# Modulation vectors summed on GpSimd instead of TensorE, and roots by Newton's steps on VectorE, in a two-layer decoder trunk

## The chip, the cores and the metric

One core of a Trainium2 chip runs the whole kernel. The metric is the device time of one execution in microseconds (us): the median of three runs, with the lowest and the highest beside it. PE is TensorE's matmul pipe, PEld its weight loads, DVE is VectorE, ACT is ScalarE, POOL is GpSimd, and SP is the engine that issues the DMAs.

## The reference

The trunk has two layers of three sublayers each, over one sequence of 256 tokens of width 1024, all in float32. Sublayers 0 and 2 of a layer are gated feed-forward products (FFN), sublayer 1 is a gMLP mixer in layer 0 and block-sparse attention in layer 1.

```
mod  = silu(c) @ mod_w[i] + mod_b[i]                 # 9 vectors of 1024 for layer i: shift, scale, gate of 3 sublayers
h    = rmsnorm(x, norm_g[i, s]) * (1 + scale) + shift
x   += 0.5 * gate * ((silu(h @ w_gate) * (h @ w_up)) @ w_out)        # s = 0, 2
x   += gate * mixer(h)                                               # s = 1
rmsnorm(x, g) = x / sqrt(mean(x*x) + 1e-6) * g
```

A vector of `mod` is the product of one row (1024 numbers) with a 1024 x 1024 matrix. There are 18 of them; each must be ready before the sublayer that uses it begins (shift, scale) or ends (gate).

## The kernel before

The 256 tokens are two tiles of 128 (t = 0 and t = 1). A float32 product is made of three float32r products: each weight tile is split on the chip into a high half (a cast on ACT) and a low half (a subtraction on DVE), and the pieces high x high, high x low and low x high are added up in PSUM. So each 128 x 1024 weight tile `hl_*` costs one cast (line 182), one subtraction (line 183) and 12 matmuls of 512 columns (line 204). The tiles `hl` share a ring of 8 buffers, so ACT and DVE can run up to 8 tiles ahead of PE and not further.

A modulation vector is a unit of background work, `mod_unit(i, s, part)`: part 0 is the shift, 1 the scale, 2 the gate. Four calls (pieces) each load 1 MB of `mod_w` and do two multiply-adds on DVE (line 117) into `ma`, a 128 x 1024 accumulator; a fifth call, `reduce`, adds up the 128 partitions of `ma` and spreads the sum over all partitions as the tile `bc`. Of the 18 vectors two are made in another way at the start of the program, which leaves 16 units. `tick` takes one call from the list `background`; `gemm` ticks after every fourth weight tile (or as its argument `ticks` says). Between the sublayers stands a hand-over: the last product's sum goes through `residual` (tiles `y`, `x`), `row_rstd` (`ss`, `mx`, the root `rx`), and `ada` (`h`), is transposed on PE (`tr_h`), and becomes `hTh` (cast, ACT) and `hTl` (subtraction, DVE), the left side of the next product. While t = 0 goes through it PE has the last 36 matmuls of t = 1; while t = 1 goes through it PE has the first matmuls of the next product for t = 0.

The program is written down in one order, and a list scheduler of the language sets the order on each engine from it. It may take an instruction that was written later if it thinks the engine free. So pieces of units that were written later stand on DVE wherever the scheduler saw room.

Of the kernel before, what the change touches and what calls it, by code (L numbers as in the profile page):

```python
# [36 lines left out]
LEAD = 6  # L37
BLOCKS = ((0, 128), (128, 128), (256, 256), (512, 256), (768, 256))
# [20 lines left out]
def trunk(ctx: ExitStack, tc: tile.TileContext, x, c, rel_bias, mod_w, mod_b, norm_g,  # L59
# [31 lines left out]
    halves_ = const.tile([P, P], F32R, name="halves")  # L91
    nc.gpsimd.memset(halves_.bitcast(F32), 0.5)
# [5 lines left out]
    def mod_unit(i, s, part):  # L98
# [22 lines left out]

        def reduce():
            hl = hl_slot([P, 2, D], F32R, f"mhl{i}{s}{part}")
            nc.scalar.copy(hl[:, 0, :], st["acc"])
            nc.vector.tensor_sub(hl[:, 1, :], st["acc"], hl[:, 0, :].bitcast(F32))
            if part == 1:
                g = pool.tile([P, 2, D], F32, tag="mraw", name=f"g{i}{s}", bufs=2)
                nc.sync.dma_start(g[:, 0, :], norm_g[i, s:s + 1, :].to_broadcast([P, D]))
            bc = pool.tile([P, D], F32, tag="bc", name=f"bc{i}{s}{part}", bufs=3)
            lhs = halves_ if part == 2 and s != 1 else ones  # L130
            for h in range(2):
                ps = tr_bank(f"mps{i}{s}{part}{h}")
                sl = slice(h * 512, h * 512 + 512)
                for j in range(2):
                    nc.tensor.matmul(ps, lhs, hl[:, j, sl], start=j == 0, stop=j == 1)  # L135
                if part == 1:
                    nc.vector.scalar_tensor_tensor(bc[:, sl], ps, 1.0, g[:, 0, sl],
                                                   op0=ALU.add, op1=ALU.mult)
                else:
                    nc.scalar.copy(bc[:, sl], ps)  # L140
            vec[i, s, part] = bc

        return [piece(k) for k in range(0, KD, 2)] + [reduce]

    vec = {}
    background = []

    def tick(n=1):
        for _ in range(n):
            if background:  # L150
                background.pop(0)()
# [5 lines left out]
    def split_weights(src, key, kt, cols):  # L157
# [25 lines left out]
        nc.vector.tensor_sub(hl[:, 1, :w], r[:, kt % 2, :w], hl[:, 0, :w].bitcast(F32))  # L183
# [90 lines left out]
    def inverse_root(m, name):  # L274
        r = small(f"r{name}")
        nc.gpsimd.tensor_tensor(r, m, mhalf, op=ALU.pow)
        return r
# [25 lines left out]
    def residual(i, s, t, ps):  # L303
        for h in range(2):
# [3 lines left out]
            nc.vector.tensor_add(x_sb[t][:, sl], x_sb[t][:, sl], y)  # L308
# [101 lines left out]
    def ffn(i, s):  # L410
# [3 lines left out]
        for n, w in enumerate((1024, 1024, 768)):  # L414
# [3 lines left out]
            else:  # L418
                g = product(w_in, f"g{i}{s}{n}", two(c0, w), h_lhs,
                            lead_first=LEAD if n == 0 else 0, lead_last=2)  # L420
# [257 lines left out]
    def gmlp(i, s):  # L678
# [282 lines left out]
```

## Time and profile before

| | us |
|---|---|
| median of 3 runs (lowest to highest) | 1143.95 (1143.52 to 1146.61) |
| time of the profiled execution | 1144.84 |
| span of the profiled execution | 1143.0 |
| PE busy | 1125.2 |
| PEld busy | 938.3 |
| DVE busy | 820.5 |
| ACT busy | 593.5 |
| POOL busy | 33.0 |

The span is what the profile covers; the time of the same execution is 1.8 us longer, and lies 0.9 us above the median of the three runs. Busy time is the union of an engine's instructions; matmuls overlap in the pipe, so PE's busy time is not a sum of their durations.

### The profile page before, as it was taken

Reading aid. Unit: us, or ns where it says so; the run is one execution under the profiler, and the core shown is the slowest. Engines: PE = TensorE matmul, PEld = TensorE weight load, DVE = VectorE, ACT = ScalarE, POOL = GpSimd, SP = SyncE. Lnnn points to the kernel's source line nnn. Section 1 sums busy time; section 2 is a strip of 40 time slices with the busy share of each in tenths; the row PEclk is TensorE's granted clock in tenths of the full one; section 3 lists DMA queues with packets and bytes.
Section 4 is the critical chain, followed back from the end, with each engine's and each line's share of the span. In section 5 each row is a group of like instructions: output and inputs, shape, how many; then the busy total and the mean of one; then the engine's idle time right before and its main releaser. Section 6 shows DMA issues by size and latency. Waiting matters only on the chain.

```text
span 1143.0 us, 14125 instructions
## 1 busy us (share of the span) xinstructions
PE 1125.2 (98%) x5429; PEld 938.3 (82%) x5429; DVE 820.5 (72%) x988; ACT 593.5 (52%) x853; POOL 33.0 (3%) x43
## 2 busy tenths in 40 slices
PE   8999999999999999999999999999999999999997
PEld 5688988778888887888988788998877778889985
DVE  3798687855797888584778867577888877644653
ACT  4565554456555544563553555455457557554541
POOL 1000000000000000000000000000000000000000
PEclk9999999999999999999999999999999999999999
DMA  9988787647698595775869558487877556455630
GB/s 315 329 312 308 284 329 276 238 155 270 230 334 318 211 337 194 289 258 174 289 254 360 175 184 308 147 323 259 292 262 271 203 184 218 151 184 158 217 141 37
DMA packets 88738, 279.47 MB, mean 244 GB/s; under 512 B 5240, under 2 KB 17616, under 8 KB 88672
## 3 DMA queue, kind: packets, MB, share of 16 engines
q1 hardware_dynamic: 88672, 278.58, 68.9%
q8 instruction: 42, 0.69, 0.2%
q14 instruction: 24, 0.20, 0.0%
HBM read 277.49 MB, written 1.07 MB: 244 GB/s over the span
## 4 chain that ended last, share of the span: by engine, by line
PE 85%; DVE 7%; DMA 3%; ACT 2%; issue 1%; POOL 1%; SPq 0%; POOLq 0%; DVEq 0%; ACTq 0%
PE ps_o L204 23%; PE ps_u L204 19%; PE ps_g L204 18%; PE ps_gu L204 6%; PE ps_v L204 5%; DMA mw<-in_mod_w_dram 3%; PE ps_qk L204 3%; PE ps_g L532 2%; PE ta L389 2%; DVE ma L117 1%; PE mps L135 1%; PE sv L750 1%; PE ps_u00b L204 1%; DVE hl_g L183 1%; PE ps_u00a L532 1%
## 5 line engine op out<-in xcount | busy, mean ns | idle before, releaser
L204 PE MATMUL ps_o<-hl_o,ahl 128*128 128x512 f32 x1440 | 334.1, 391 | 1.0 <-ACT ahl L345 1.0
L204 PEld LDWEIGHTS ps_o<-hl_o,ahl 128*128 128x128 f32 x1440 | 269.1, 188 | 56.3 <-ACT ahl L345 1.2
L182 ACT CAST hl_o<-raw_o 128x1024 fp32r<-128x1024 f32 x120 | 125.7, 1055 | 112.1 <-PE ps_o L204 71.8
L183 DVE TENSOR_TENSOR hl_o<-raw_o,hl_o 128x1024 fp32r<-128x1024 f32 x120 | 145.9, 1222 | 52.7 <-ACT hl_o L182 51.9
L204 PE MATMUL ps_g<-hl_g,hTh 128*128 128x512 f32 (+1 forms) x704 | 183.4, 371 | 0.0
L204 PE MATMUL ps_u<-hl_u,hTh 128*128 128x512 f32 (+1 forms) x704 | 181.5, 369 | 0.0
L117 DVE SCALAR_TENSOR_TENSOR ma<-mw,cs,ma 128x1024 f32<-128x1024 f32 x128 | 165.5, 1294 | 17.5 <-DMA mw<-in_mod_w_dram 16.9
L204 PEld LDWEIGHTS ps_u<-hl_u,hTh 128*128 128x128 f32 x704 | 129.6, 188 | 17.6
L204 PEld LDWEIGHTS ps_g<-hl_g,hTh 128*128 128x128 f32 x704 | 129.2, 188 | 17.5 <-ACT hTh L285 0.2
L183 DVE TENSOR_TENSOR hl_u<-raw_u,hl_u 128x1024 fp32r<-128x1024 f32 (+1 forms) x88 | 98.4, 1126 | 60.0 <-ACT hl_u L182 58.8
L183 DVE TENSOR_TENSOR hl_g<-raw_g,hl_g 128x1024 fp32r<-128x1024 f32 (+1 forms) x88 | 97.6, 1124 | 50.8 <-ACT hl_g L182 50.5
L182 ACT CAST hl_g<-raw_g 128x1024 fp32r<-128x1024 f32 (+1 forms) x88 | 83.3, 974 | 94.8 <-PE ps_u L204 84.1
L182 ACT CAST hl_u<-raw_u 128x1024 fp32r<-128x1024 f32 (+1 forms) x88 | 85.3, 974 | 59.1 <-PE ps_g L204 54.6
L204 PE MATMUL ps_g<-hl_g,hTl 128*128 128x512 f32 (+1 forms) x352 | 110.3, 372 | 0.0
L204 PE MATMUL ps_u<-hl_u,hTl 128*128 128x512 f32 (+1 forms) x352 | 108.6, 369 | 0.0
L204 PEld LDWEIGHTS ps_u<-hl_u,hTl 128*128 128x128 f32 x352 | 65.4, 188 | 8.7
L204 PEld LDWEIGHTS ps_g<-hl_g,hTl 128*128 128x128 f32 x352 | 65.0, 188 | 9.1 <-issue 0.6
L204 PE MATMUL ps_gu<-hl_gu,hTh 128*128 128x512 f32 x192 | 55.0, 394 | 0.0
L204 PE MATMUL ps_v<-hl_v,hTh 128*128 128x512 f32 x192 | 54.2, 392 | 0.3 <-ACT hl_v L182 0.3
L183 DVE TENSOR_TENSOR hl_v<-raw_v,hl_v 128x1024 fp32r<-128x1024 f32 x24 | 28.8, 1221 | 22.7 <-ACT hl_v L182 22.7
L204 PEld LDWEIGHTS ps_v<-hl_v,hTh 128*128 128x128 f32 x192 | 35.8, 188 | 8.4 <-ACT hl_v L182 0.5
L204 PEld LDWEIGHTS ps_gu<-hl_gu,hTh 128*128 128x128 f32 x192 | 35.8, 188 | 7.1
(173 smaller groups left out, 1249.0 us busy)
## 6 DMA issues: line engine op xcount, KB each, us to landing
mw<-in_mod_w_dram SPq DMA_DIRECT2D x64, 1024.0 KB, 7.1
raw_o<-in_ffn_w_out_dram SPq DMA_DIRECT2D x44, 1024.0 KB, 4.8
raw_g<-in_ffn_w_in_dram SPq DMA_DIRECT2D x28, 1024.0 KB, 5.1
raw_u<-in_ffn_w_in_dram SPq DMA_DIRECT2D x28, 1024.0 KB, 5.0
raw_g<-in_ffn_w_in_dram SPq DMA_DIRECT2D x16, 768.0 KB, 4.5
raw_u<-in_ffn_w_in_dram SPq DMA_DIRECT2D x16, 768.0 KB, 4.4
raw_v<-in_gmlp_w_in_dram SPq DMA_DIRECT2D x12, 1024.0 KB, 7.7
raw_gu<-in_gmlp_w_in_dram SPq DMA_DIRECT2D x12, 1024.0 KB, 7.1
```

The source lines that it names most:

```text
L117: nc.vector.scalar_tensor_tensor(st["acc"], w[:, j, :], cs[:, k0 + j:k0 + j + 1], st["acc"], op0=ALU.mult, op1=ALU.add)
L135: nc.tensor.matmul(ps, lhs, hl[:, j, sl], start=j == 0, stop=j == 1)
L182: nc.scalar.copy(hl[:, 0, :w], r[:, kt % 2, :w])
L183: nc.vector.tensor_sub(hl[:, 1, :w], r[:, kt % 2, :w], hl[:, 0, :w].bitcast(F32))
L204: nc.tensor.matmul(ps[t, h][:, :cw], lhs(k, t)[p], hls[k][:, wp, o:o + cw], start=k == 0 and p == 0 and wp == 0, stop=k == nk - 1 and p == 1)
L389: nc.tensor.transpose(ps[:, j * P:(j + 1) * P], src[:, j * P:(j + 1) * P], ident)
L532: nc.tensor.matmul(prod[n][t, h], h_lhs(k, t)[part], hls[n, k][:, wp, h * 512:h * 512 + 512], start=k == 0 and part == 0 and wp == 0, stop ...
L750: nc.tensor.matmul(sv[:, sl], wsT[:, g, :], v[n][:, t, lo - n * D:hi - n * D], start=True, stop=True)
```

## The change

Of the 16 reductions over partitions, 13 go from TensorE to GpSimd: two `partition_all_reduce` instructions of 128 x 512 each read `ma` and write `bc`, in place of a cast on ACT, a subtraction on DVE, four matmuls with a matrix of ones, and two copies out of PSUM. For the scale (part 1) one multiply-add on DVE follows, over 128 x 1024. The three units named in `ON_PE` keep the matmuls; they are the ones that are worked on within the attention. The factor 0.5 of the FFN gates moves from the matrix of halves into `residual`.

The root `1/sqrt` was a power on GpSimd (line 276). It stays so at the program's two ends (`AT_ENDS`); the other 12 become eight small DVE instructions: a first guess from the bits, and three Newton steps.

No unit is ticked in the first product after a hand-over (`ticks=KD + 1`, in FFNs and the gMLP), and the DVE instructions of the 13 units may not stand ahead of the latest weight split written before them (`issue_after`), while those of the three other units may.

```diff
+ON_PE = ((1, 1, 2), (1, 2, 0), (1, 2, 1))
+AT_ENDS = ("x000", "x001", "fin0", "fin1", "last")
...
         def reduce():
+            bc = pool.tile([P, D], F32, tag="bc", name=f"bc{i}{s}{part}", bufs=3)
+            for h in range(2):
+                sl = slice(h * 512, h * 512 + 512)
+                nc.gpsimd.partition_all_reduce(bc[:, sl], st["acc"][:, sl], P, ReduceOp.add)
+            if part == 1:
+                nc.vector.scalar_tensor_tensor(bc, bc, 1.0, norm_row(), op0=ALU.add, op1=ALU.mult)
+            vec[i, s, part] = bc
+
+        def reduce_pe():
             hl = hl_slot([P, 2, D], F32R, f"mhl{i}{s}{part}")
             nc.scalar.copy(hl[:, 0, :], st["acc"])
             nc.vector.tensor_sub(hl[:, 1, :], st["acc"], hl[:, 0, :].bitcast(F32))
...
-        return [piece(k) for k in range(0, KD, 2)] + [reduce]
+        pe = (i, s, part) in ON_PE
+        return [(f, not pe) for f in
+                [piece(k) for k in range(0, KD, 2)] + [reduce_pe if pe else reduce]]
...
             if background:
-                background.pop(0)()
+                f, held_back = background.pop(0)
+                with ExitStack() as stack:
+                    if held_back:
+                        stack.enter_context(tc.issue_after(split["last"].ins))
+                    f()
...
-        nc.vector.tensor_sub(hl[:, 1, :w], r[:, kt % 2, :w], hl[:, 0, :w].bitcast(F32))
+        split["last"] = nc.vector.tensor_sub(hl[:, 1, :w], r[:, kt % 2, :w],
+                                             hl[:, 0, :w].bitcast(F32))
...
     def inverse_root(m, name):
-        r = small(f"r{name}")
-        nc.gpsimd.tensor_tensor(r, m, mhalf, op=ALU.pow)
+
+        if name in AT_ENDS:
+            r = small(f"r{name}")
+            nc.gpsimd.tensor_tensor(r, m, mhalf, op=ALU.pow)
+            return r
+        r, mh, t = (small(f"{a}{name}") for a in ("r", "mh", "rt"))
+        nc.vector.tensor_scalar(r.bitcast(I32), m.bitcast(I32), -0.5, float(0x5F3759DF),
+                                op0=ALU.mult, op1=ALU.add)
+        nc.vector.tensor_scalar_mul(mh, m, -0.5)
+        for _ in range(3):
+            nc.vector.scalar_tensor_tensor(t, r, mh, r, op0=ALU.mult, op1=ALU.mult)
+            nc.vector.scalar_tensor_tensor(r, t, 1.5, r, op0=ALU.add, op1=ALU.mult)
         return r
...
-            nc.vector.tensor_add(x_sb[t][:, sl], x_sb[t][:, sl], y)
+            nc.vector.scalar_tensor_tensor(x_sb[t][:, sl], y, 0.5 if s != 1 else 1.0,
+                                           x_sb[t][:, sl], op0=ALU.mult, op1=ALU.add)
...
-                            lead_first=LEAD if n == 0 else 0, lead_last=2)
+                            lead_first=LEAD if n == 0 else 0, lead_last=2,
+                            ticks=4 if n else KD + 1)
```

The order on GpSimd, in the gMLP and the FFN after it (layer 0; the first digit in a name is the layer, the second the sublayer, the third the part or the tile). Before:

```order
L106 MEMSET ma012_1877 128x1024
L106 MEMSET ma020_2304 128x1024
L276 TENSOR_TENSOR rx010_1749<-mx010_1747,mhalf_82 128x1
L276 TENSOR_TENSOR rx011_1834<-mx011_1832,mhalf_82 128x1
L686 AFFINE_SELECT ws_2050<-ws_2050 128x2048
```

And after the change, where each `ISA` row with `bc` is a pair of all-reduces:

```order
L133 ISA bc011_1642<-ma011_1385 128x512 x2
L108 MEMSET ma020_2471 128x1024
L720 AFFINE_SELECT ws_2029<-ws_2029 128x2048
L133 ISA bc012_2416<-ma012_2066 128x512 x2
L108 MEMSET ma021_3043 128x1024
L133 ISA bc020_2886<-ma020_2471 128x512 x2
```

The powers are gone from the queue, and every unit's accumulator is cleared only after the pair of the unit two before it, whose buffer it takes over.

On DVE, at the hand-over into the attention (from layer 1's first FFN to its sublayer 1; `y10`, `x1` are residuals of the FFN, `h11`, `rx11`, `hl_qk0` belong to the attention's first product). Before, from the first residual of t = 0 to its `h`:

```order
L307 TENSOR_TENSOR y1000_6357<-ps_o10_00_5987,bc102_5383 128x512
L308 TENSOR_TENSOR x0_69<-x0_69,y1000_6357 128x512
L117 SCALAR_TENSOR_TENSOR ma120_6558<-mw1206_6731,cs_71,ma120_6558 128x1024 x2
L307 TENSOR_TENSOR y1001_6360<-ps_o10_01_5993,bc102_5383 128x512
L293 TENSOR_TENSOR h1100_6365<-x0_69,bc111_6197 128x512
L308 TENSOR_TENSOR x0_69<-x0_69,y1001_6360 128x512
L293 TENSOR_TENSOR h1101_6367<-x0_69,bc111_6197 128x512
L307 TENSOR_TENSOR y1010_6446<-ps_o10_10_5998,bc102_5383 128x512
L271 SCALAR_TENSOR_TENSOR mx110_6375<-ssx1100_6369,ssx1101_6372 128x1
L308 TENSOR_TENSOR x1_70<-x1_70,y1010_6446 128x512
L298 SCALAR_TENSOR_TENSOR h1100_6365<-h1100_6365,rx110_6377,bc110_5770 128x512
```

After, the end of the same piece (12 rows; three of the multiply-adds of unit (1, 1, 2) and `mx110` stand ahead of them, behind `y1001`):

```order
L339 TENSOR_TENSOR y1010_6421<-ps_o10_10_5961,bc102_5512 128x512
L307 SCALAR_TENSOR_TENSOR rtx110_6345<-rx110_6343,mhx110_6344 128x1
L204 TENSOR_TENSOR hl_qk0_2_6418<-raw_qk0_2_6415,hl_qk0_2_6418 128x1024
L308 SCALAR_TENSOR_TENSOR rx110_6343<-rtx110_6345,rx110_6343 128x1
L340 SCALAR_TENSOR_TENSOR x1_70<-y1010_6421,x1_70 128x512
L307 SCALAR_TENSOR_TENSOR rtx110_6345<-rx110_6343,mhx110_6344 128x1
L204 TENSOR_TENSOR hl_qk0_3_6502<-raw_qk0_2_6415,hl_qk0_3_6502 128x1024
L308 SCALAR_TENSOR_TENSOR rx110_6343<-rtx110_6345,rx110_6343 128x1
L339 TENSOR_TENSOR y1011_6424<-ps_o10_11_5964,bc102_5512 128x512
L307 SCALAR_TENSOR_TENSOR rtx110_6345<-rx110_6343,mhx110_6344 128x1
L340 SCALAR_TENSOR_TENSOR x1_70<-y1011_6424,x1_70 128x512
L308 SCALAR_TENSOR_TENSOR rx110_6343<-rtx110_6345,rx110_6343 128x1
```

Then follow `h1110` and `h1100`. So the row `y1011`, which reads the last sum of t = 1, now stands ahead of the `h1100` of t = 0.

On PE at the same hand-over, around the transposes `tr_h11` of t = 0. Before:

```order
L204 MATMUL ps_o10_11_6001<-hl_o10_19_6301,ahl18_6321 128x512
L283 MATMUL tr_h1100_6380<-ident_73,h1100_6365 128x128 x4
L204 MATMUL ps_o10_11_6001<-hl_o10_19_6301,ahl18_6321 128x512
L283 MATMUL tr_h1101_6388<-ident_73,h1101_6367 128x128 x4
L204 MATMUL ps_o10_11_6001<-hl_o10_19_6301,ahl18_6321 128x512
L204 MATMUL ps_o10_11_6001<-hl_o10_20_6306,ahl20_6330 128x512 x3
L204 MATMUL ps_o10_11_6001<-hl_o10_21_6309,ahl20_6330 128x512 x3
L204 MATMUL ps_qk0_00_6490<-hl_qk0_0_6434,hTh_6363 128x512 x2
```

After:

```order
L226 MATMUL ps_o10_11_5964<-hl_o10_19_6261,ahl18_6287 128x512 x3
L226 MATMUL ps_o10_11_5964<-hl_o10_20_6272,ahl20_6296 128x512 x3
L226 MATMUL ps_o10_11_5964<-hl_o10_21_6275,ahl20_6296 128x512 x3
L315 MATMUL tr_h1100_6355<-ident_73,h1100_6331 128x128 x4
L315 MATMUL tr_h1101_6363<-ident_73,h1101_6333 128x128 x4
L226 MATMUL ps_qk0_00_6474<-hl_qk0_0_6409,hTh_6329 128x512 x2
```

The eight matmuls of the old product that stood behind the first transpose now stand ahead of it, and the next product follows the transposes at once. For t = 1 the transposes moved back too, from behind 35 matmuls of the next product to behind 42. At the four other hand-overs the transposes of t = 0 stand one matmul from the old product's end, and those of t = 1 behind 47 matmuls of the next product.

## Rows read from the trace of the kernel before

**Rows 1.** The page: engines (busy, share, instructions), granted clock in 40 slices.
```profile
PE 1125.2 (98%) x5429; PEld 938.3 (82%) x5429; DVE 820.5 (72%) x988; ACT 593.5 (52%) x853; POOL 33.0 (3%) x43
...
PEclk9999999999999999999999999999999999999999
```

**Rows 2.** Waits of PE: waiter, released by, us in total, times, longest.
```profile
PE tr_h L283 <- DVE h L298: 3.3, 8, 0.7
```

**Rows 3.** Timeline of PE within layer 0's first output product.
```profile
164.83 35.52 PE L204 MATMUL ps_o<-hl_o,ahl 128*128 128x512 f32 x156
```

**Rows 4.** Waits of ACT and DVE for weight tiles of the output products.
```profile
ACT hl_o L182 <- PE ps_o L204: 71.8, 53, 1.7
...
DVE hl_o L183 <- ACT hl_o L182: 51.9, 63, 1.8
```

**Rows 5.** Groups by line: the reductions (busy, mean ns, idle before).
```profile
L135 PE MATMUL mps<-mhl,ones 128*128 128x512 f32 x48 | 13.3, 394 | 0.0
L135 PE MATMUL mps<-mhl,halves 128*128 128x512 f32 x16 | 4.3, 393 | 0.0
L125 DVE TENSOR_TENSOR mhl<-ma,mhl 128x1024 fp32r<-128x1024 f32 x16 | 19.6, 1224 | 13.6 <-ACT mhl L124 13.5
```

**Rows 6.** Timeline of PE around one reduction: start, us, engine, line.
```profile
150.54 1.10 PE L135 MATMUL mps<-mhl,ones 128*128 128x512 f32 x4
151.48 0.52 PE L204 MATMUL ps_u<-hl_u,hTh 128*128 128x384 f32 x2
```

**Rows 7.** Timelines of POOL and DVE, and one group of POOL by shape.
```profile
225.65 1.22 DVE L183 TENSOR_TENSOR hl_v<-raw_v,hl_v 128x1024 fp32r<-128x1024 f32 x1
225.88 1.40 POOL L276 TENSOR_TENSOR rx<-mx,mhalf 128x1 f32<-128x1 f32 x1 [9.80 <-DVE mx L271]
...
235.64 4.22 DVE L117 SCALAR_TENSOR_TENSOR ma<-mw,cs,ma 128x1024 f32<-128x1024 f32 x2
236.75 2.04 POOL L686 TENSOR_SCALAR_AFFINE_SELECT ws<-ws 128x2048 f32<-128x2048 f32 x1 [9.47 <-DMA ws<-in_gmlp_w_s_dram]
...
masks.py:199 POOL TENSOR_SCALAR_AFFINE_SELECT ident<-ident 128x128 f32<-128x128 f32 x1 | 0.3, 293 | 0.0
```

**Rows 8.** Groups of DVE: small and wide multiply-adds.
```profile
L117 DVE SCALAR_TENSOR_TENSOR ma<-mw,cs,ma 128x1024 f32<-128x1024 f32 x128 | 165.5, 1294 | 17.5 <-DMA mw<-in_mod_w_dram 16.9
...
L271 DVE SCALAR_TENSOR_TENSOR mx<-ssx,ssx 128x1 f32<-128x1 f32 x12 | 1.8, 154 | 5.1 <-ACT junkx L267 5.0
```

**Rows 9.** Timeline of the hand-over into the attention.
```profile
809.95 1.28 DVE L117 SCALAR_TENSOR_TENSOR ma<-mw,cs,ma 128x1024 f32<-128x1024 f32 x1 [0.75 <-DMA mw<-in_mod_w_dram]
811.15 1.22 DVE L183 TENSOR_TENSOR hl_qk<-raw_qk,hl_qk 128x1024 fp32r<-128x1024 f32 x1
...
818.78 0.69 DVE L307 TENSOR_TENSOR y<-ps_o,bc 128x512 f32<-128x512 f32 x1
819.38 0.68 DVE L293 TENSOR_TENSOR h<-x,bc 128x512 f32<-128x512 f32 x1
...
822.82 0.92 POOL L276 TENSOR_TENSOR rx<-mx,mhalf 128x1 f32<-128x1 f32 x1 [40.74 <-DVE mx L271]
823.78 1.41 DVE L298 SCALAR_TENSOR_TENSOR h<-h,rx,bc 128x512 f32<-128x512 f32 x2 [0.44 <-POOL rx L276]
824.59 0.66 PE L283 MATMUL tr_h<-ident,h 128*128 128x128 f32 x4 [0.51 <-DVE h L298]
...
825.11 2.35 DVE L183 TENSOR_TENSOR hl_qk<-raw_qk,hl_qk 128x1024 fp32r<-128x1024 f32 x2
...
825.43 1.11 ACT L285 CAST hTh<-tr_h 128x512 fp32r<-128x512 f32 x2
...
835.88 0.63 PE L283 MATMUL tr_h<-ident,h 128*128 128x128 f32 x4 [0.34 <-DVE h L298]
```

**Rows 10.** Windows: length, busy of PE, PEld, DVE, ACT, POOL; gMLP gating.
```profile
295.00:376.00 81.00, 80.01 (x401) 67.50 (x400) 70.46 (x93) 41.57 (x55) 2.37 (x2) 1.00 0.81 299
```

More of the change, by code (lines that the diff above doesn't have):

```diff
@@ L9 @@
 from concourse._compat import with_exitstack
+from concourse.bass_isa import ReduceOp
 from concourse.masks import make_identity
@@ L13 @@
 F32R = mybir.dt.float32r
+I32 = mybir.dt.int32
 AF = mybir.ActivationFunctionType
@@ L90, in trunk @@
     nc.gpsimd.memset(ones.bitcast(F32), 1.0)
-    halves_ = const.tile([P, P], F32R, name="halves")
-    nc.gpsimd.memset(halves_.bitcast(F32), 0.5)
     mhalf = const.tile([P, 1], F32, name="mhalf")
@@ L120, in piece, with norm_row @@
             return f
+        def norm_row():
+            g = pool.tile([P, 2, D], F32, tag="mraw", name=f"g{i}{s}", bufs=2)
+            nc.sync.dma_start(g[:, 0, :], norm_g[i, s:s + 1, :].to_broadcast([P, D]))
+            return g[:, 0, :]
         def reduce():
+            bc = pool.tile([P, D], F32, tag="bc", name=f"bc{i}{s}{part}", bufs=3)
[6 more added lines that the diff above has]
+        def reduce_pe():
             hl = hl_slot([P, 2, D], F32R, f"mhl{i}{s}{part}")
@@ L126, in reduce @@
             if part == 1:
-                g = pool.tile([P, 2, D], F32, tag="mraw", name=f"g{i}{s}", bufs=2)
-                nc.sync.dma_start(g[:, 0, :], norm_g[i, s:s + 1, :].to_broadcast([P, D]))
+                g = norm_row()
             bc = pool.tile([P, D], F32, tag="bc", name=f"bc{i}{s}{part}", bufs=3)
-            lhs = halves_ if part == 2 and s != 1 else ones
             for h in range(2):
@@ L134, in reduce @@
                 for j in range(2):
-                    nc.tensor.matmul(ps, lhs, hl[:, j, sl], start=j == 0, stop=j == 1)
+                    nc.tensor.matmul(ps, ones, hl[:, j, sl], start=j == 0, stop=j == 1)
                 if part == 1:
-                    nc.vector.scalar_tensor_tensor(bc[:, sl], ps, 1.0, g[:, 0, sl],
+                    nc.vector.scalar_tensor_tensor(bc[:, sl], ps, 1.0, g[:, sl],
                                                    op0=ALU.add, op1=ALU.mult)
@@ L141, in reduce @@
             vec[i, s, part] = bc
-        return [piece(k) for k in range(0, KD, 2)] + [reduce]
+        pe = (i, s, part) in ON_PE
+        return [(f, not pe) for f in
+                [piece(k) for k in range(0, KD, 2)] + [reduce_pe if pe else reduce]]
     vec = {}
+    split = {}
     background = []
@@ L706, in gmlp @@
             interleave(gemm(w_in, f"v{n}", two(GM + n * D, D), h_lhs, g,
-                            lead_first=LEAD if n == 0 else 0, lead_last=2),
+                            lead_first=LEAD if n == 0 else 0, lead_last=2,
+                            ticks=4 if n else KD + 1),
                        {2: [(prepare,)]} if n == 1 else {})
```

## The prediction

> **What bounds the kernel now.** I read the page first [rows 1]: PE is busy in 98% of the span, with its clock at the higher level, 2.4 GHz, in every slice, DVE in 72%, POOL in 3%. Then the waits of PE [rows 2]: inside the program only the transposes `tr_h` of the hand-overs make it wait, 3.3 us in 8 waits. So PE is the bound, and a matmul that leaves its queue is time gained one for one. The timeline of a steady stretch gives its pace [rows 3]: 156 matmuls of 512 columns in 35.52 us, the last one 0.39 us long, so 35.13 / 155 = 0.2266 us from start to start, 2.72 us for a weight tile of 12. The waits of ACT and DVE [rows 4] show how far they are ahead: ACT waits for PE to free a buffer of the ring (71.8 us) and DVE for ACT (51.9 us). The ring of 8 is full most of the time, and DVE can lose time without PE noticing, as long as the loss stays below the tiles it is ahead.
>
> **What the change takes from PE.** The 64 matmuls of the reductions have 13.3 + 4.3 us of PE's busy time [rows 5]. One reduction's four start at 150.54 and the next matmul at 151.48 [rows 6]: 0.94 us, or 12.2 us for the 13 that go. Nothing covers them, so 12.2 us come off the end. DVE loses 13 subtractions (1.224 us each [rows 5], 15.9 us) and ACT its casts and copies; both are ahead of PE, so I count that as nothing by itself.
>
> **What an all-reduce costs.** The trace has none. Two bounds come from the one instruction of POOL that reads a wide tile, at two sizes [rows 7]: 2.04 us for 2048 columns, 0.293 us for 128, so 0.91 us per 1000 columns and 0.18 us fixed. One pass over 512 columns is 0.64 us, the lower bound. Adding up the 128 partitions one after the other is 128 passes of 0.46 us, 59 us, the upper bound. Between them, halving 128 seven times is 0.18 + 7 x 0.46 = 3.4 us. I take 3.4: it needs the fewest passes that reach all partitions, and POOL's other rows run at the speed of single passes.
>
> The Trainium skill (GPSIMD Engine Reference, Cross-partition — where GPSIMD wins) measured a partition-axis `tensor_reduce` of [128, 2048] at 247.7 us, an estimate of 62 us for a half; by it the 26 halves would be 1610 us. No row of this trace shows it, and the instruction is another one. By 3.4 us the 26 halves are 88 us of an idle engine; the upper bound is a rival below.
>
> **What it costs DVE.** POOL and DVE block each other. The wide POOL instruction starts at 236.75 while DVE does two multiply-adds of 1.29 us [rows 7, 8]: those two take 4.22 us together, 1.6 us too long, which is about what is left of POOL's 2.04 us. The other way round, the power of one column at 225.88 takes 1.40 us, with DVE in a subtraction until 226.87 [rows 7]; elsewhere it takes 0.92 [rows 9]. Both DVE instructions read two SBUF tiles, as most of DVE's work here does. So each half stops DVE for about 3.4 us: 26 x 3.4 = 88 us, of 1143 - 820 = 322 us in which it is idle. Spread out, that is hidden by the ring. Where DVE is already full it is not; so I budget each hand-over.
>
> DVE's prices from the timeline [rows 9]: a wide row in a busy stretch 1.14 us (two subtractions in 2.35) or 1.20 (a multiply-add, 809.95 to 811.15), any row of 512 columns 0.60 (818.78 to 819.38), a row of one column 0.15 [rows 8].
>
> *An ordinary hand-over* (the four others). From the first tile of the output product to the first `h` of t = 0, the new order holds 25 subtractions, 8 multiply-adds, one over `bc`, 20 rows of 512 and 9 small ones: 28.5 + 9.6 + 1.2 + 12.0 + 1.4 = 52.7 us. PE's time for the 22 tiles is 59.8 us. Up to 13.9 us of DVE's rows (8 tiles, 2 multiply-adds, 4 others) can be done before PE begins. The pair at the product's end adds 6.8 us, one at its start at most as much: 38.8 + 13.6 = 52.4, so DVE is in time, and the first `h` waits for PE as it did. Newton's eight rows take 1.2 us in place of a power of 0.9 to 1.4 us and its handing over, but `y`, `x` and a subtraction now stand between them; the transposes of t = 0 moved back to meet that, and what covered the cast to `hTh` (two in 1.11 us [rows 9]) has gone ahead of them. I charge 0.4 us for each, 1.6 us in all.
>
> *The hand-over into the attention.* The units kept on PE are not held behind the weight splits, and their multiply-adds stand in the chain. To the first `h` DVE has 26 subtractions, 16 multiply-adds, one over `bc`, 23 rows of 512 and 9 small ones: 29.6 + 19.2 + 1.2 + 13.8 + 1.4 = 65.2 us, less 13.9 is 51.3, and with 6.8 to 13.6 us of all-reduces 58 to 65, against 59.8 on PE. So DVE is late by 0 to 5 us. Besides, `y1011` stands ahead of `h1100` and needs the last matmul of the old product. From that end E: `y1011`, `x1`, `h1110` and `h1100` take 0.6 + 0.7 + 0.6 + 0.75 and their latencies, about 3.0 us. I take E + 4. PE then transposes, and waits 0.8 us more for `hTh`, uncovered: 4.8 us idle, against 0.51 before [rows 9], so +4.3. For t = 1, the rows from there to `h1110` are 3 subtractions, one of the kept units', 4 multiply-adds, 5 rows of 512 and 9 small ones, 13.8 us; PE has 1.2 us until the product starts and 42 matmuls, 9.5 us. The rest, 3.1 us, it waits; before it was 0.34 [rows 9]. +2.8. What is late next are the attention's own tiles on DVE, which the ring covers.
>
> *Elsewhere.* The gMLP's gating is DVE's fullest stretch, 70.5 of 81 us [rows 10]. Four halves add 13.6, and some six multiply-adds fewer stand in it (7.2 us): 77 of 81. I charge 0.8 us for gating rows that wait behind a stop of 3.4 us. The gate's factor in `residual` is a multiply-add in place of an addition, within the 0.60. The last powers stay on POOL; nothing is ahead of them in its queue for tens of us.
>
> **Sum.** -12.2 + 1.6 + 4.3 + 2.8 + 0.8 = -2.7 us. The profiled execution took 1144.84, so 1142.1 by its measure; it lay 0.9 us above the median of the runs, so 1141.2 by the median. I say 1141.4.
>
> **The rivals.**
>
> A. *The hand-over into the attention costs little.* If DVE comes through its rows quicker than I priced them (gaps in it filled by rows that I counted in sequence), PE waits there 1 to 3 us, not 7. For it: the list has a weight tile or multiply-add between almost any two of Newton's steps, and PE still has its old cover for half of t = 0. Against it: `y1011` ahead of `h1100`, which no speed of DVE gets round. -12.2 + 2 + 1.6 + 0.8 gives 1136, and 1132 with nothing lost anywhere.
>
> B. *An all-reduce is longer than 5 us*, with DVE stopped as long; slower. At 6 us the attention's hand-over has 51.3 + 18 = 69 us for DVE against 59.8, 5 us more than I charged, and with 3 us at the others the sum is +5: 1149. At 8 us: 51.3 + 24 = 75 is 11 more, and the three other hand-overs that end with such a pair have 38.8 + 24 = 63 against 59.8, 3 us each: +18, 1162. It decides from about 5 us. For it: bounds of 0.64 and 59 us. Against it: only that fewer passes are possible.
>
> C. *A serial walk*: 128 passes, 59 us a half. 26 x 59 = 1534 us make POOL the bound, and with DVE stopped meanwhile the kernel takes about 1534 plus the 820 us of DVE, less what does not read two tiles: over 2000. For it no row, against it the same argument as for B. The figure that the Trainium skill (GPSIMD Engine Reference, Cross-partition — where GPSIMD wins) has for a reduction over partitions would be this case.
>
> D. *DVE falls short in the gating or within the attention*, where its load rises to 95%: +3 to +6 us over my sum, 1144 to 1147.
>
> **How the numbers follow.** Less than 0.3% (3.4 us) is about what this kernel's measurement cannot tell from no change: "same" is 1140.5 to 1147.4. My forecast has 0.42 (its own range 1138 to 1146; 0.12 of it faster, 0.28 same, 0.02 slower), A 0.30 (0.28 faster), B 0.18 (0.15 slower), C 0.04, D 0.06 (0.04 same). Together: faster 0.40, same 0.37, slower 0.23. The range leaves out C, B beyond 7 us (0.07) and A at its best (0.07): 1134 to 1154.
>
> **What would show it.** PE's matmuls of the reductions must fall from 64 to 12. POOL's all-reduces, by start to start within a pair, must be near 3.4 us, and a two-input DVE row beside them that much longer. PE's waits for `tr_h` must rise from 3.3 us to about 12, with 4 to 5 us in one wait at the attention's first transpose and 3 at the second. If those two are under 1 us, A holds; if the pair is over 10 us and PE waits for weight splits at the ends of the FFNs, B. I would be wrong altogether if DVE went on beside the all-reduces undisturbed, and most exposed where I priced a DVE row by row without letting it fill its gaps.

## The result, and the profile after

The changed kernel takes 1137.91 us (median of 5 runs, 1137.30 to 1139.20). The kernel before, beside it on the same chip, takes 1144.28, and the ratio is 0.9944 (95% interval 0.9933 to 0.9954). So it is faster by 0.56%, 6.4 us. The forecast was 1141.4 with a range of 1134 to 1154. The profiled execution has a span of 1137.3 us and a time of 1139.17, 1.3 above the median (before: 0.6 above the 1144.28), so the two profiles differ by 5.7 us where the medians differ by 6.4. One of the five runs of the kernel before took 1246.84 us; the other four lie between 1143.52 and 1146.61, and by their median, 1144.12, the gain is 6.2 us.

The page of the changed kernel, engines and granted clock; then its waits of PE and two of its groups (answers to [rows 1, 2, 5]):

```profile
PE 1115.5 (98%) x5377; PEld 930.3 (82%) x5377; DVE 859.0 (76%) x1067; ACT 572.6 (50%) x822; POOL 114.3 (10%) x56
...
PEclk9999999999999999999999999999899999999999
```
```profile
PE tr_h L315 <- DVE h L330: 7.5, 2, 6.4
```
```profile
L149 PE MATMUL mps<-mhl,ones 128*128 128x512 f32 x12 | 3.9, 408 | 0.0
...
L133 POOL PARTITION_ALL_REDUCE bc<-ma x26 | 93.0, 3624 | 742.3 <-DVE ma L119 700.1 <-ACT hl_o L203 42.2
```

PE has 52 matmuls fewer, DVE is 38.5 us busier, although 13 subtractions are gone. The waits of PE for `h` went from 3.3 us in 8 places to 7.5 us in 2: the ordinary hand-overs lost theirs, and the attention's has one of 6.4 us. The one slice of the clock row below 9 is at that place.

To see where the time went I compared the start of each matmul of the program, in PE's order, before and after. PE has 5332 matmuls besides the reductions and the filler at the start, as many in both kernels, and for each reduction matmul that stands ahead 0.235 us (a quarter of the 0.94 in [rows 6]) is taken off. What is left grows only where PE waits more, and falls where it waits less. I call this the ledger; all its numbers are after minus before, in us, so a gain has a minus:

| place | forecast | ledger |
|---|---|---|
| 52 matmuls off PE | -12.2 | -12.2 |
| program start | 0 | -0.35 |
| ordinary hand-overs: into gMLP, FFN, FFN, FFN | +1.6 | -0.67 -0.19 -0.55 -0.04 = -1.45 |
| gMLP, gating | +0.8 | -0.32 |
| hand-over into the attention, t = 0 and t = 1 | +7.1 | +8.6 |
| the rest | 0 | +0.05 |
| sum | -2.7 | -5.7 |

The ends of PE's work differ by 5.67 us, as the sum says. The 0.35 of the program's start is no effect of the change: in the runs below the same start differs from that of the kernel before by -0.5 to +0.6. The timelines of POOL and DVE around one pair of all-reduces in the output product (start, us, engine, line):

```profile
183.38 3.32 DVE L204 TENSOR_TENSOR hl_o<-raw_o,hl_o 128x1024 fp32r<-128x1024 f32 x1 [0.17 <-ACT hl_o L203]
186.61 2.76 DVE L379 TENSOR_TENSOR ahl<-act,ahl 128x512 fp32r<-128x512 f32 x1
...
186.51 3.31 POOL L133 PARTITION_ALL_REDUCE bc<-ma  x1
```

The all-reduce shown takes 3.31 us (the mean of all 26 is 3.62), and a DVE row that reads two SBUF tiles and falls into it lasts nearly as long: 2.76 us for a row of 512 columns that takes 0.68 elsewhere. PE saw nothing of it here. The hand-over into the attention, PE and then DVE (answers to [rows 9]):

```profile
810.76 1.75 PE L226 MATMUL ps_o<-hl_o,ahl 128*128 128x512 f32 x7
818.94 1.94 PE L315 MATMUL tr_h<-ident,h 128*128 128x128 f32 x8 [6.43 <-DVE h L330]
820.70 2.07 PE L226 MATMUL ps_qk<-hl_qk,hTh 128*128 128x512 f32 x4
...
832.46 1.29 PE L315 MATMUL tr_h<-ident,h 128*128 128x128 f32 x8 [1.04 <-DVE h L330]
```
```profile
799.88 1.28 DVE L119 SCALAR_TENSOR_TENSOR ma<-mw,cs,ma 128x1024 f32<-128x1024 f32 x1 [2.55 <-DMA mw<-in_mod_w_dram]
...
810.73 0.15 DVE L293 SCALAR_TENSOR_TENSOR mx<-ssx,ssx 128x1 f32<-128x1 f32 x1
810.85 1.28 DVE L119 SCALAR_TENSOR_TENSOR ma<-mw,cs,ma 128x1024 f32<-128x1024 f32 x1
812.05 0.15 DVE L303 TENSOR_SCALAR rx<-mx 128x1 int32<-128x1 int32 x1
...
812.90 1.22 DVE L204 TENSOR_TENSOR hl_qk<-raw_qk,hl_qk 128x1024 fp32r<-128x1024 f32 x1
...
814.84 1.22 DVE L204 TENSOR_TENSOR hl_qk<-raw_qk,hl_qk 128x1024 fp32r<-128x1024 f32 x1
...
816.04 0.69 DVE L339 TENSOR_TENSOR y<-ps_o,bc 128x512 f32<-128x512 f32 x1
...
818.04 1.41 DVE L330 SCALAR_TENSOR_TENSOR h<-h,rx,bc 128x512 f32<-128x512 f32 x2
```

The old product ends at 812.51. DVE has no gap from 799.88 on, where it had waited 2.55 us for the data of a multiply-add. From `mx` (810.73) to `h` of t = 0 (818.04) it needs 7.3 us: one multiply-add, then Newton's eight steps with two weight splits and rows of t = 1 between them. The row `y` that needs the last sum (`y1011`) comes at 816.04, 3.5 us after that sum is there, and `h` of t = 0 behind it. PE idles 6.43 us, and then runs at little over half its clock, near the lower level of 1.2 GHz, as the windows of the same kernel show (length, busy of PE, PEld, DVE, ACT, POOL, then the granted clock):

```profile
820.00:823.00 3.00, 3.00 (x11) 2.35 (x10) 3.00 (x6) 2.31 (x6) 0.00 (x0) 0.56 0.14 52
823.00:826.00 3.00, 3.00 (x15) 2.47 (x14) 3.00 (x6) 0.00 (x0) 0.95 (x1) 1.00 0.00 1
```

The first six matmuls of the product take 2.37 us (820.70 to 823.07) in place of 1.36, so the idle time cost 1 us more than itself. At an ordinary hand-over of the same kernel the transposes of both token tiles wait for nothing:

```profile
214.69 0.63 PE L315 MATMUL tr_h<-ident,h 128*128 128x128 f32 x4
...
226.88 1.12 PE L315 MATMUL tr_h<-ident,h 128*128 128x128 f32 x8
```

### The profile page after: what moved, and what is told of

It reads as the page before. It is cut to its first block, busy times and chain, and to the rows that moved or that the text cites. A ratio compares the mean times of both kernels' runs of the same rounds, so it can differ in the third digit from the quotient of the medians.

```text
span 1137.3 us, 14085 instructions
## 1 busy us (share of the span) xinstructions
PE 1115.5 (98%) x5377; PEld 930.3 (82%) x5377; DVE 859.0 (76%) x1067; ACT 572.6 (50%) x822; POOL 114.3 (10%) x56
## 4 chain that ended last, share of the span: by engine, by line
PE 89%; DVE 4%; ACT 2%; DMA 2%; issue 2%; SPq 0%; POOLq 0%; POOL 0%; DVEq 0%; ACTq 0%
PE ps_o L226 25%; PE ps_g L226 19%; PE ps_u L226 19%; PE ps_v L226 6%; PE ps_gu L226 6%; PE ps_g L566 2%; PE ta L422 2%; DMA mw<-in_mod_w_dram 2%; PE ps_qk L226 1%; PE ps_vv L226 1%; PE sv L785 1%; PE ps_u00b L226 1%; DVE ma L119 1%; PE ps_u00a L566 1%; PE tr_h L315 1%
## 5 line engine op out<-in xcount | busy, mean ns | idle before, releaser
L204 DVE TENSOR_TENSOR hl_o<-raw_o,hl_o 128x1024 fp32r<-128x1024 f32 x120 | 157.0, 1319 | 43.4 <-ACT hl_o L203 43.0
L133 POOL PARTITION_ALL_REDUCE bc<-ma x26 | 93.0, 3624 | 742.3 <-DVE ma L119 700.1
L204 DVE TENSOR_TENSOR hl_u<-raw_u,hl_u 128x1024 fp32r<-128x1024 f32 (+1 forms) x88 | 113.3, 1306 | 49.8 <-ACT hl_u L203 48.7
L379 DVE TENSOR_TENSOR ahl<-act,ahl 128x512 fp32r<-128x512 f32 x44 | 42.4, 970 | 12.1 <-ACT ahl L378 12.0
```

The costliest lines, as they stand in the source:

```text
L133: nc.gpsimd.partition_all_reduce(bc[:, sl], st["acc"][:, sl], P, ReduceOp.add)
L204: split["last"] = nc.vector.tensor_sub(hl[:, 1, :w], r[:, kt % 2, :w], hl[:, 0, :w].bitcast(F32))
L379: nc.vector.tensor_sub(v[:, 1], a[:, k0:k0 + 2, :], v[:, 0].bitcast(F32))
```

## The experiments

Theory T, after the result: the sums on GpSimd are hidden but for the attention hand-over, and there the multiply-adds of the unit (1,1,2), which may run ahead of weight splits, make DVE late. Its rivals are that Newton's steps do it, or the stops by the all-reduces. The first four kernels:

**1. All units held back** (`e1_hold_all`), an edit to the changed kernel:

```diff
-        return [(f, not pe) for f in
+        return [(f, True) for f in
```

> The only edit to the changed kernel: the three units that stay on TensorE are held behind the weight splits like the others. Theory T: the 6.4 us wait for the first transpose of the attention hand-over, and the 1.5 us of low clock behind it, come from the four multiply-adds of unit (1,1,2) that may run ahead there; now that chain has none of them, so the wait falls below 0.5 us and the time to about 1130 us (1129 to 1131.5). Rival R1: the wait comes from Newton's steps themselves, which put y1011 ahead of h1100; then 1136 to 1139, with over 4 us still waited. Rival R2: the multiply-adds only move, and make PE wait inside the attention's products instead: 1133 to 1138 with the wait in other rows.

Measured: 1138.71 us (1137.70 to 1139.57), ratio to the kernel before 0.9951 (0.9937 to 0.9966): no gain. Its waits of PE:

```profile
PE ps_qk L226 <- DVE hl_qk L204: 3.6, 2, 2.7
PE tr_h L315 <- DVE h L330: 2.8, 1, 2.8
```

The wait of 6.4 us is gone, and 6.4 us of others stand in its place, for two weight splits and for the second `h`. The ledger loses 9.4 us at this hand-over. So T as I put it falls, and R2's mechanism holds (the time lies 0.7 us above its range): held back, the multiply-adds make PE wait at later rows of the same hand-over. This run does not show whether they alone are the cause; runs 3, 6 and 11 bear on Newton's steps, R1.

**2. Sums back on TensorE** (`e2_sums_on_pe`): `reduce_pe` for all 16 units, all else as changed.

```diff
-                [piece(k) for k in range(0, KD, 2)] + [reduce_pe if pe else reduce]]
+                [piece(k) for k in range(0, KD, 2)] + [reduce_pe]]
```

> The changed kernel with all 16 sums by matmuls of ones again; Newton's steps, the holding back of 13 units and the ticks stay. Theory T: the all-reduces cost nothing that PE notices, so this undoes exactly the 52 matmuls, 12.2 us: 1149 to 1151 us, slower than the kernel before by 5 to 7, with the long wait at the attention hand-over still there. Rival R3: the stops of DVE by the all-reduces (26 of 3.3 us) are part of why DVE is late at the attention hand-over; then that wait falls to 1 to 3 us and the time is 1143 to 1147.

Measured: 1150.36 us (1149.61 to 1150.93), ratio 1.0053 (1.0036 to 1.0069), 12.4 above the changed kernel. The long wait is still there:

```profile
PE tr_h L315 <- DVE h L330: 5.4, 1, 5.4
```

The stops by the all-reduces therefore cost PE about 1 us at the attention (ledger +7.7 there against +8.6) and 1 us in the gating, and no more than 0.1 us at an ordinary hand-over. T holds here, and R3 falls.

**3. Newton's steps alone** (`e3_before_newton`): the kernel before, with the new `inverse_root` and nothing else.

> The kernel before with one edit: 12 roots by Newton's steps on VectorE, in place of powers on GpSimd. My forecast charged each ordinary hand-over +0.4 us; the trace of the changed kernel shows -0.4 to -0.7 each. Theory T: that gain belongs to Newton's steps (the transposes move back behind other matmuls and no longer wait), and at the attention hand-over, where y1011 stands ahead of h1100 here too but no multiply-add of unit (1,1,2) does, PE waits 3 to 5 us: in all 1144 to 1147. Rival R1 (Newton alone makes the wait of 6 us and the clock drop): 1148 to 1151. Rival R4: the ordinary gain comes from the missing ticks, not from Newton: the waits of tr_h stay at 3 us outside the attention.

Measured: 1169.48 us (1168.33 to 1170.48), ratio 1.0220 (1.0205 to 1.0236): far slower than any of the expectations. PE and DVE at the hand-over into the gMLP:

```profile
216.62 1.75 PE L206 MATMUL ps_o<-hl_o,ahl 128*128 128x512 f32 x7
224.03 1.97 PE L295 MATMUL tr_h<-ident,h 128*128 128x128 f32 x8 [5.67 <-DVE h L310]
```
```profile
216.22 1.28 DVE L119 SCALAR_TENSOR_TENSOR ma<-mw,cs,ma 128x1024 f32<-128x1024 f32 x1 [0.29 <-DMA mw<-in_mod_w_dram]
217.43 0.21 DVE L287 SCALAR_TENSOR_TENSOR rtx<-rx,mhx 128x1 f32<-128x1 f32 x1
217.56 1.22 DVE L185 TENSOR_TENSOR hl_v<-raw_v,hl_v 128x1024 fp32r<-128x1024 f32 x1
...
220.03 0.68 DVE L319 TENSOR_TENSOR y<-ps_o,bc 128x512 f32<-128x512 f32 x1
...
223.23 1.41 DVE L310 SCALAR_TENSOR_TENSOR h<-h,rx,bc 128x512 f32<-128x512 f32 x2
```

The eight steps need about 1.4 us, but between them stand multiply-adds, weight splits and the residual of the other token tile: 7.5 us from the first step (215.73) to `h`. The ledger loses 5 to 7 us here and at three more hand-overs (into layer 0's second FFN, layer 1's first and the attention), 24 us in all. So the gain at the ordinary hand-overs is not of Newton's steps, as theory T had it, and at the attention's they cost 5.8 us with no all-reduce in the kernel, which is a part of R1. In the changed kernel the same steps cost nothing at the ordinary hand-overs; so holding back or the missing ticks make up for them.

**4. Nothing held back** (`e4_no_hold`): the first edit with `False` for `True`.

> The changed kernel with no unit held back (no issue_after around the background work). In the order of DVE the attention hand-over then has no multiply-add in the chain to the first h, and the transposes stand as at the ordinary hand-overs. Theory T: the attention wait goes as in the first run of this call, and what the holding back buys elsewhere is small: 1130 to 1133. Rival R5: without it, multiply-adds and the stops by the all-reduces get ahead of weight splits, and PE waits for splits or for h at other places: 1135 to 1145.

Measured: 1188.62 us (1185.03 to 1190.19), ratio 1.0384 (1.0364 to 1.0403). T was wrong about how little the holding back is worth: 51 us. The attention hand-over itself lost only 0.6 us in the ledger, but three of the ordinary ones 12 to 14 each, the last 4.5, the gating 9, and an FFN 4. R5 named such waits at other places, but its 1135 to 1145 is 44 us short. Waits of PE:

```profile
PE tr_h L315 <- DVE h L330: 24.3, 7, 8.3
```

Theory T2, formed from these: a hand-over has no room on DVE for multiply-adds, wherever the scheduler puts them, and it is the ticks in the first product that bring them there. The change took these ticks away in the FFNs and the gMLP and left one after every tile in the attention's first product.

**5. Fewer multiply-adds in the attention hand-over** (`e5_early`): the first edit, and

```diff
-                        early=early, after_first=first)
+                        early=early, after_first=first,
+                        ticks=3 if (i, s) == (1, 0) else 4)
...
-                u = product(w_in, f"u{i}{s}{n}", two(FF + c0, w), h_lhs, lead_last=2)
+                u = product(w_in, f"u{i}{s}{n}", two(FF + c0, w), h_lhs, lead_last=2,
+                            ticks=2 if (i, s, n) == (1, 0, 0) else 4)
...
-        interleave(gemm(*firsts[i, s], h_lhs, qk, lead_first=LEAD, lead_last=2, ticks=1,
+        interleave(gemm(*firsts[i, s], h_lhs, qk, lead_first=LEAD, lead_last=2, ticks=2,
...
+            if (i, s) == (1, 0):
+                background += nxt[:4]
+                nxt = nxt[4:]
```

> As the first run (all units held back), and the four pieces of unit (1,1,2) are ticked in layer 1's first FFN (a tick after every second tile of its first up product and after every third of its output product), and the attention's first product ticks after every second tile. Theory T2, formed after the first run: the attention hand-over loses 8 us because DVE has too many rows there, wherever they stand; this takes away four multiply-adds before the second h and about ten more up to the end of the product. Then the waits of PE for h and for hl_qk fall from 6.4 us in all to under 1.5 and the time to 1129 to 1132. Rival R6: the rows moved make PE wait in the FFN, or later in the attention: 1135 to 1139 with the waits in other rows.

Measured: 1135.82 us (1135.12 to 1137.03), ratio 0.9925 (0.9910 to 0.9939). The time lies in R6's range, but only 1.1 us of the loss is in the FFN that took the unit, as R6 has it; the ledger still loses 4.75 us at the hand-over (waits of 2.2, 0.7 and 1.1). Four multiply-adds, now of unit (1,2,0), still stand between the `h` of t = 0 and that of t = 1 there.

**6. All roots as powers** (`e6_pow_all`): `if True:` in place of `if name in AT_ENDS:`.

> The changed kernel with all 14 roots as powers on GpSimd, the sums on GpSimd too. Its queue then alternates between powers and all-reduces, with a load instruction at every change of kind (14 of them, against 2). Theory T: the loads lie in the chain of the hand-overs and cost microseconds each: over 1145, with waits for tr_h far above the 3.3 us of before. Rival R7: a load is cheap or is done ahead of time: the transposes stand nearly as before, 1130 to 1136, and Newton's steps are not needed.

Measured: 1141.86 us (1140.53 to 1143.72), ratio 0.9975 (0.9964 to 0.9986). Neither expectation: at the ordinary hand-overs the ledger gains as much as with Newton's steps (-0.70, -0.23, -0.56), and the attention's loses 3.7 in place of 8.6. Apart from the program's start, what this kernel loses against the changed one is in one place, the first root of the gating (7.6 us in the ledger there). POOL, DVE and the waits of PE there, and last POOL's waits ahead of the same powers in the kernel before:

```profile
285.16 0.95 POOL L108 MEMSET ma<- 128x1024 f32 x1
294.92 0.59 POOL L300 TENSOR_TENSOR rv<-vt,mhalf 128x1 f32<-128x1 f32 x1 [8.81 <-issue]
...
285.86 0.15 DVE L760 TENSOR_SCALAR vt<-vt 128x1 f32<-128x1 f32 x1
...
PE ps_gu L226 <- DVE hl_gu L204: 6.6, 1, 6.6
```
```profile
POOL rv L276 <- DVE vt L725: 20.9, 2, 15.7
```

The number is ready at 286.0 and the power starts at 294.92; POOL is idle for 8.81 us with nothing shown that it waits for. In its queue a load instruction (`MODIFY_POOL_CONFIG`, which the timelines leave out; the trace has it at 286.1, and 13 pairs of it in this run against 3 in the changed kernel, not 14 and 2) stands between the all-reduces and the power. In the kernel before, with no all-reduce ahead, both such powers wait for DVE's number and for nothing else. So the gap goes with the change from all-reduces to a power; that the load fills it is argued from its place, since no row has the load's length. At the hand-overs that have such a change, POOL waits another 18.9 to 24.0 us for DVE's number, and nothing is lost.

**7. Holding back alone** (`e7_before_hold`): the kernel before, with `issue_after` on all background work.

> The kernel before with one edit: the background work of all 16 units held behind the latest weight split. Theory T3: holding back helps only where Newton's steps would be spread out by multiply-adds; with powers it buys at most 1 us at the four ordinary hand-overs, and at the attention the rows of unit (1,1,2) crowd t = 1: 1143 to 1149. Rival R8: the gain of 1.7 us at the ordinary hand-overs in the changed kernel is of the holding back: 1140 to 1142.

Measured: 1152.86 us (1152.24 to 1154.10), ratio 1.0074 (1.0059 to 1.0089). The ordinary hand-overs lose 0.2 to 1.0 us each, the attention's 4.2 and its products 1.7 more. R8 falls; T3's direction holds, and the time is above its range. Held back, the multiply-adds of a first product crowd t = 1: three stand ahead of a weight split of the attention's first product, for which PE waits 2.3 us.

**8. Ticks as before** (`e8_ticks4`): `ticks=4` in the first products of the FFNs and the gMLP, all else as changed.

> The changed kernel with the ticks of the first product after a hand-over as before (every fourth tile). Two multiply-adds then stand ahead of each second h of a hand-over, and the transposes of t = 1 two matmuls earlier; at the attention the first tiles of unit (1,2,0) stand where unit (1,1,2) stood. Theory T: DVE has room there (42 matmuls of cover, 9.5 us): 1136 to 1140. Rival R9: the missing ticks are what takes the waits from the second transposes: 0.5 to 1.5 us at each of four hand-overs, 1140 to 1144.

Measured: 1159.98 us (1156.12 to 1162.57), ratio 1.0142 (1.0125 to 1.0159): 22 us above the changed kernel, far beyond both. The profiled execution is the fastest of the four, so the ledger shows 17 us of them. In it each ordinary hand-over loses 3.5 to 5.7 us. DVE and PE at the hand-over into the gMLP:

```profile
219.82 1.28 DVE L119 SCALAR_TENSOR_TENSOR ma<-mw,cs,ma 128x1024 f32<-128x1024 f32 x1
...
224.94 0.73 PE L226 MATMUL ps_v<-hl_v,hTh 128*128 128x512 f32 x2 [0.92 <-DVE hl_v L204]
...
230.96 1.29 PE L315 MATMUL tr_h<-ident,h 128*128 128x128 f32 x8 [2.06 <-DVE h L330]
```

Four multiply-adds, 5 us of DVE, stand between the first `h` and the second; my expectation counted two and only the cover of the second transposes, not the splits that the product itself needs.

**9. No tick in the attention's first product** (`e9_early_clear`): the fifth kernel with `ticks=KD + 1` there, and a tick after every tile of the last attention product (`vv`).

> As the fifth run (all units held back, unit (1,1,2) ticked in layer 1's first FFN), and no tick at all in the attention's first product, as in every other first product after a hand-over; the last attention product ticks after every tile instead. Theory T2: what the fifth run still waited at the attention hand-over (2.2 + 0.7 for weight splits, 1.1 for h) was multiply-adds in that product; now the order of DVE there is that of the ordinary hand-overs, and PE's ledger loses under 0.5 us there: 1130 to 1133. Rival R6: the multiply-adds moved into the last attention product make its tiles late: 1134 to 1138.

Measured: 1130.22 us (1129.90 to 1130.72), ratio 0.9870 (0.9855 to 0.9885). The ledger now gains 0.15 us at the attention hand-over, and PE's transposes there wait for next to nothing:

```profile
813.21 0.63 PE L315 MATMUL tr_h<-ident,h 128*128 128x128 f32 x4
...
825.97 1.29 PE L315 MATMUL tr_h<-ident,h 128*128 128x128 f32 x8 [0.17 <-DVE h L330]
```

T2 holds, and this kernel is faster than both, 14 us below the one before.

**10. The last three sums on GpSimd too** (`e10_early_clear_pool`): the ninth kernel with `ON_PE = ()`.

> The run above with the last three sums on GpSimd too (no matmuls of ones left). PE has 12 matmuls fewer, 2.8 us. Theory T: with room made for DVE around the hand-over, six more stops of 3.3 us in the attention are hidden: 2 to 3 us below the run above, 1127.5 to 1130.5. Rival R2b: DVE, 85 to 95% busy in the attention's products, can't take 20 us of stops there: PE waits for weight splits or for the softmax's rows, and the time is not below that of the run above.

Measured: 1137.82 us (1136.40 to 1138.52), ratio 0.9934 (0.9921 to 0.9946): 7.6 above the ninth, with 2.8 us less on PE. R2b holds. The sum of unit (1,1,2) falls into the hand-over (POOL, DVE, PE):

```profile
815.61 6.49 POOL L133 PARTITION_ALL_REDUCE bc<-ma  x2 [53.23 <-DVE y L339]
...
816.03 2.37 DVE L340 SCALAR_TENSOR_TENSOR x<-y,x 128x512 f32<-128x512 f32 x1
818.32 3.33 DVE L325 TENSOR_TENSOR h<-x,bc 128x512 f32<-128x512 f32 x2
...
822.84 0.96 PE L226 MATMUL ps_qk<-hl_qk,hTh 128*128 128x512 f32 x3 [2.81 <-DVE hl_qk L204]
```

Three rows of 512 columns take 5.5 us, and the next weight split is late by 2.8. The ledger loses 3.3 us here and 5.2 in the attention's products.

**11. Newton's steps in the gating alone** (`e11_pow_not_v`): the changed kernel with `if name[0] != "v":` for the power.

> The changed kernel with the roots of the hand-overs by powers on GpSimd and only the two roots of the gMLP's gating by Newton's steps. In the run with all powers the one great loss was in the gating (6.6 us of wait for a weight split, 8.3 us in PE's ledger); the hand-overs cost 0.4 us each more than with Newton's steps, the attention's about 5 less. Theory T4: the two losses are independent; without the gating's this gives 1141.9 - 8.3 = 1133.6, 1132 to 1135, less than the changed kernel: Newton's steps pay in the gating alone. Rival R10: the loss in the gating came from something else (library loads moved, the order of the weight splits) and stays: 1138 to 1142.

Measured: 1131.13 us (1130.47 to 1133.46), ratio 0.9883 (0.9867 to 0.9898). T4 holds, with a time 0.9 us below its range: the gating's loss is gone, and the attention hand-over's is 1.8 us in place of 8.6. At the ordinary hand-overs the ledger is that of the changed kernel within 0.03 us; the 0.4 us more that this expectation charges them is not there. The waits, and DVE at the attention hand-over:

```profile
PE tr_h L315 <- DVE h L330: 4.3, 6, 2.3
```
```profile
808.85 0.15 DVE L293 SCALAR_TENSOR_TENSOR mx<-ssx,ssx 128x1 f32<-128x1 f32 x1
...
810.74 1.42 DVE L330 SCALAR_TENSOR_TENSOR h<-h,rx,bc 128x512 f32<-128x512 f32 x2 [0.49 <-POOL rx L300]
```

From `mx` to `h` of t = 0 DVE needs 1.9 us, with one multiply-add between, where the changed kernel needs 7.3; the multiply-adds ahead of `mx` are the same, and DVE waited there for data as well (1.83 us). So in the changed kernel Newton's steps, and the rows put between them, make 6.9 of the 8.6 us: R1 holds for the larger part, and T2 is narrowed: with powers the same multiply-adds cost 1.8 us there.

**12. The price of an all-reduce** (`e12_sizes`): the changed kernel with other sizes in five units.

> The changed kernel with all-reduces of other sizes in five units, to price the instruction: two of 1024 columns in unit (0,0,2) (the second repeats the first), four of 256 in (0,1,1), eight of 128 in (0,2,0), and in (1,0,1) and (1,2,2) two more of 64 and of 32 partitions ahead of the two whole ones. Start to start within a series. The prediction's formula, 0.18 us fixed and as many passes of 0.91 us per 1000 columns as halvings: 6.7 us for 1024 columns, 1.8 for 256, 1.0 for 128; 2.9 us for 64 partitions (six passes), 2.5 for 32 (five). Rival F: a fixed cost of about 1 us and the rest by columns, whatever the partitions: about 5.6, 2.2 and 1.6, and 3.3 for both smaller counts. Rival W: proportional to the partitions: 1.7 and 0.9. The time is not compared (up to 5 us of more stops).

Measured, of each series one of the shorter ones (1024, 256 and 128 columns; 512 columns of 64 and of 32 partitions); others last longer, up to 2.73 us for 256 columns:

```profile
96.69 6.50 POOL L137 PARTITION_ALL_REDUCE bc<-ma  x1
183.43 1.80 POOL L137 PARTITION_ALL_REDUCE bc<-ma  x1 [42.21 <-ACT hl_o L208]
350.48 1.15 POOL L137 PARTITION_ALL_REDUCE bc<-ma  x1
594.67 3.31 POOL L137 PARTITION_ALL_REDUCE bc<-ma  x1
996.15 3.31 POOL L137 PARTITION_ALL_REDUCE bc<-ma  x1
```

By columns the formula is near (6.7, 1.8 and 1.0 forecast); by partitions it is wrong: 64 and 32 take as long as 128, as rival F has it, whose prices by columns are wrong; rival W falls. The time was 1138.11 us in one run.

## Why the prediction came out as it did

**What bounds, and what PE saves:** right. With 0.235 us for each of the 52 matmuls the ledger stays level between the hand-overs, and putting them back costs 12.4 us by the medians and 11.1 by the profiled spans (run 2), where the stops of DVE go too.

**The all-reduce:** 3.4 us forecast, 3.31 measured, which rules out rivals B and C. The size was right, and in part by luck: the time goes with the columns, about 6.2 us per 1000 ((6.50 - 3.31) / 0.512), but there is not one pass per halving of the partitions, from which the 3.4 was worked out (run 12).

**The stops of DVE:** right where wide rows that read two SBUF tiles meet an all-reduce, and right that the ring hides most of them: run 2 shows about 1 us at the attention and 1 us in the gating. The 88 us of stops were twice too many: DVE is busy 859.0 us, and 833.0 in run 2 with 13 subtractions (15.9 us) more, so the stops made its rows longer by an estimated 42 us. The gating, charged 0.8 us for its stops, came out 0.3 better than before.

**The ordinary hand-overs, "0.4 us for each, 1.6 us in all":** this is the term that was mis-sized, by sign too. They gained 1.45 us. I had counted what the new order adds and given nothing for what it takes out: the four multiply-adds of the first product. Runs 8 and 7 show the parts: with the ticks back each loses 3.5 to 5.7 us, and held back with ticks and powers 0.2 to 1.0. Run 6 gains the same with powers as the change does with Newton's steps, and run 2 with the sums on PE, so the gain is of the missing ticks together with the holding back. Missing ticks without holding back were run only together with Newton's steps (run 4, 51 us slower), not with powers.

**The attention hand-over, +7.1:** measured +8.6. The place was right, and that DVE is late and `y1011` stands ahead of `h`. The sharing out was not: Newton's steps, with the splits and the rows of t = 1 between them, make 6.9 of the 8.6 us (run 11), where I had 4.3 for `y1011`; the kept units' multiply-adds are the other condition, for with Newton's steps and none of them there the loss is gone too (run 9). I had taken `h` at E + 4, from the rows that follow the last sum, beside "late by 0 to 5 us"; the two add up. DVE was 3.5 us late and then needed its 3 us, and PE waited 6.4 us, not 4.8. The low clock behind it, 1 us, was not in the sum. t = 1 waited 1.04 us, where I had 3.1: PE had come that much later itself.

**The sum:** -5.7 in place of -2.7, of which the ordinary hand-overs are 3.0, the gating 1.1, the start 0.35, and the attention 1.5 the other way. The time lies nearer to rival A's 1136 than to my 1141.4, but A's mechanism, a cheap attention hand-over, is not what happened. Rival D did not come either: from the hand-over to the attention's output product the ledger is level within 0.1 us. The forecast's own range of 1138 to 1146 is just missed, at 1137.91, and that the time came so near is in part luck: the attention's error has the other sign than the rest. The waits of PE for `h` were to rise to about 12 us, with 4 to 5 in one and 3 in another; they rose to 7.5, with 6.4 and 1.0.

Not settled: why the sums on GpSimd cost 5.2 us in the attention's products in run 10, row by row, and what the gains of runs 9 and 11 would be together, which was not run, nor was a hand-over with its data there in time (the 2.55 us).

## What to carry to other kernels

Work that is hidden on the average is not hidden at a hand-over: price each from the last sum that it needs, add what the engine is late to the rows that must follow, and look at which fill-in work the code issues there. Steps of a short chain on a busy, list-scheduled engine cost what the scheduler puts between them, not their own length: eight steps of 1.4 us took 7.5 alone (run 3) and 7.3, from `mx`, at the attention (the change), and nothing extra where no fill-in work was issued beside them. Of the change's parts the sums on GpSimd are worth 12.4 us (run 2); Newton's steps pay in the gating alone, and with powers at the hand-overs the kernel is 6.8 us faster than the change (run 11). When a change moves one kind of work with several guards, take each guard away by itself: here holding back was worth 51 us and the missing ticks 22, more than the move (12). These are prices within the changed kernel; holding back alone made the kernel before 8 us slower (run 7). Run 9, which gives the second guard to the place that lacked it (with all units held back and one moved ahead), is 7.7 us faster than the change.

## What the hardware showed that was not expected

- A partition all-reduce of 512 columns takes 3.31 us for 128, 64 and 32 partitions alike, and 6.50 for 1024 columns. The Trainium skill (GPSIMD Engine Reference, Cross-partition — where GPSIMD wins) has 247.7 us for a reduction over partitions of [128, 2048] with another instruction, by which 512 columns would be an estimated 62 us; the measurement decides, and that figure does not hold for this instruction.
- Small rows of DVE go through during an all-reduce. In the changed kernel's gating the second of a pair fills POOL until 286.3, and Newton's steps beside it keep their length:

```profile
278.95 7.34 POOL L133 PARTITION_ALL_REDUCE bc<-ma  x2 [44.92 <-DVE ma L119]
...
285.41 0.22 DVE L307 SCALAR_TENSOR_TENSOR rtv<-rv,mhv 128x1 f32<-128x1 f32 x1
```

- The change from all-reduces to a power on GpSimd kept POOL idle for 8.81 us with no row for it (run 6). The Trainium skill (GPSIMD Engine Reference, Instruction dispatch) tells of a load of some 6 us at the first call to new code, with no visible instruction. The idle time here is longer, if it is that load; no row has its length.
- PE's granted clock was 0.56, near the lower level of 1.2 GHz, from 820 to 823 us, behind the wait of 6.43 us, and 1.00 in the 3 us after.
